# Modulation sums moved beside the merge, the attention's slots filled in another order, and three hand-overs and the first loads reordered

## The chip, the cores and the metric

The kernel runs on one core of a Trainium2 chip. The metric is device time in microseconds (us) of one launch; before the change it is 2489.1 us, the median of 3 runs (2488.27 to 2489.74). The core's engines run in parallel, each through its own list of instructions in order: PE (TensorE: matmuls), DVE (VectorE), ACT (ScalarE), POOL (GpSimd), and SP, which here only issues DMA transfers. An instruction that waits for another engine holds everything behind it on its own engine.

## The reference, cut to what matters

One layer over 512 latent tokens of width 1024, with 256 context tokens that share all weights:

```
mx = (silu(c) @ w_ada + b_ada)                     # six modulation vectors: sh1, sc1, g1, sh2, sc2, g2
px = split((x * (1 + sc1) + sh1) @ w_in)           # all input projections; pc the same for the context
ox_hg  = HGRN2 recurrence over 8 heads             # branch A
ox_cv  = Conformer convolution, 31 taps            # branch B
qx, kx = rope(rms_norm(q)), rope(rms_norm(k))      # branch C: 8 query heads, 4 key/value heads
ox_att = softmax(q k^T / sqrt(128)) v              # over 512 + 256 keys
mix = (sig(z0) * hg_out(ox_hg) + sig(z1) * conv_out(ox_cv) + sig(z2) * (ox_att @ w_att_o)) @ w_out
x = LN(alpha * x + g1 * mix)
q = (x * (1 + sc2) + sh2) @ wq                     # PEER: top 16 of 128 + 128 keys, 8 heads
act = gelu(u_tab[expert] . x);  y = sum(gate * act * v_tab[expert])
x = LN(alpha * x + g2 * y)
```

Of the modulation vectors, sh1 and sc1 are needed at the start; g1, sh2, sc2 and g2 only after the attention.

## The kernel before, in words

Every product is done in float32 as three passes over a weight split in two parts: `wload` starts a 512 KB transfer into `wraw` (three buffers in rotation), ACT writes the upper part `whi` in two halves, and DVE or POOL subtracts it to give the lower part `wlo`. `mm3` then issues three matmuls per 128 rows (lines L142 to L144), so a product of 512 columns has 24 matmuls.

The order of weights is one list, `todo`, filled by `want(...)`. `fetch_next()` takes the next entry, if fewer than three stand ready, and issues its load and its conversion at that place of the program; `feed(...)` hands over the first that is ready, and if there is none it issues the load and the conversion on the spot. An entry `('ada', a)` is a load alone, of 512 KB of the transposed `w_ada`: it takes a `wraw` buffer until it is used.

The stages, in order of time:

- Start (0 to 39 us): sh1 and sc1 from `w_ada`, by matmuls; loads on SP's queue, small constants on ACT's.
- HGRN2 heads and convolution (to about 600 us), then norm and the first output product with its gate.
- The merge loop (656 to 744 us), 8 steps `j`: a gate product `('in', Z_MG + KT + j)`, a sigmoid on ACT, a product `('conv', j)`, a multiplication on DVE (`ms`), an addition on POOL (`mix`).
- Attention (745 to about 1062 us): 32 slots, one for each of 8 heads and 4 blocks of queries. `slot(n, early, late, mid)` does in this order: softmax scaling of slot n (`P`), the softmax of n+1, the scores of n+2 (`S`), the steps in `early`, the transposes of `P` (`pt`), the steps in `late`. The steps fill PE's time with the projections of the next group's heads: `key`, `value` and `query` are generators whose `yield` marks where a step ends. A group is 8 slots (two query heads over one key head): g = 0, 1, 2 prepare the next, g = 3 computes the third branch's merge gates instead (`mgate`).
- Into the same slots the modulation sums are dealt: `adas()` multiplies a 128x1024 piece of `w_ada` with silu(c) and adds it up on DVE, one instruction for each of 32 pieces, plus an addition of the bias after every four.
- Output projection, PEER queries and top-k (`decodes` and `best` on DVE), with dense products of the expert table as filler (`next_item`). `SUBS` says which engine makes `wlo` for which table.
- Gate loop (1445 to 1640 us): one-hot matrices on DVE, matmuls `pg`, dense products as filler from a generator `run`. Then the dense stage (1656 to 2430 us): `weigh(n)` multiplies activations and gates, split in `ph` and `pl`, and products add up into `acc`.

PSUM tiles named `mm` come from a pool of two in the attention: a third one waits until the first has been read.

Of the kernel before, what the change touches and what calls it, by code (L numbers as in the profile page):

```python
# [94 lines left out]
def body(tc, I, O):  # L95
# [65 lines left out]
    nc.scalar.dma_start(cc, I['cc'])  # L161
    nc.scalar.dma_start(bada, I['b_ada'])
    A.activation(silc, cc, AF.Sigmoid)
# [44 lines left out]
    hgn = cst.tile([128, 1], F32, name="hgn")  # L208
    nc.scalar.dma_start(hgn, I['hg_g'])
    dw = cst.tile([128, KT, 31], F32, name="dw")  # L210
    nc.scalar.dma_start(dw, I['dw'])
    chan = {}
    for n in ('cb', 'clg', 'clb'):
        chan[n] = cst.tile([128, KT], F32, name=n)
        nc.scalar.dma_start(chan[n], I[n])
    hcs = ExitStack()
# [32 lines left out]
    def want(*ws):  # L249
        for w in ws:  # L250
            todo.append(w)

    def run(*gens):
        for g in gens:
            for _ in g:
                pass
# [36 lines left out]
    want(('in', Z_G + H - 1), ('in', Z_MG + 6), ('in', Z_MG + 7))  # L293
    want(*[('hg', j) for j in range(KT)])
    for j in range(KT):
        want(('in', Z_MG + KT + j), ('conv', j))
    want(*[('in', z) for z in (Z_AK, Z_AQ, Z_AV, Z_AQ + 1)])
# [344 lines left out]

    for t in (0, 0, 0, 0, 1, 0, 1, 0, 1, 0):
        next(first[t])
    lbl = cst.tile([128, 2, H], F32, name="lbl")
    nc.scalar.dma_start(lbl, I['lbl'])
# [91 lines left out]
    for j in range(KT):  # L738
# [8 lines left out]
        go(ln)  # L747
    run(ln)
    for j in range(KT):
        ps = pmm.tile([128, T], F32, name="mm")  # L750
        p_ = product(ps, feed('in', Z_MG + KT + j), xhl, 4)
        go(p_)
        fetch_next()
        go(p_)
        s = mp.tile([128, T], F32, name="ms", bufs=2)
        A.activation(s, ps, AF.Sigmoid)
        ps = pmm.tile([128, T], F32, name="mm")
        p_ = product(ps, feed('conv', j), uhl, 4)
        go(p_)
        fetch_next()  # L760
        go(p_)
        fetch_next()
        V.tensor_mul(s, ps, s)
        G.tensor_add(mix[j], mix[j], s)
# [57 lines left out]
    NS = NB + NBC  # L822
    steps = [a for j in range(32) for a in ((j,) if j % 4 < 3 else (j, None))]
    for g in range(3):
        for n, z in ((0, Z_AK + g + 1), (2, Z_AQ + 2 * g + 2), (3, Z_AV + g + 1), (2, Z_AQ + 2 * g + 3), (3, None)):
            want(*[('ada', a) for a in steps[:n] if a is not None])
            del steps[:n]
            if z is not None:
                want(('in', z))
    mg = [('in', Z_MG + 16 + j) for j in range(KT)]  # L830
    for n, m in ((2, 0), (3, 1), (3, 2), (2, 3)):
        want(*[('ada', a) for a in steps[:n] if a is not None])
        del steps[:n]
        want(*(mg[m:m + 1] if m < 3 else mg[3:]))
    want(*[('att', j) for j in range(KT)], ('u', 0))
# [6 lines left out]
    def key(g):  # L842
# [15 lines left out]
        for (x, n, o_), (zg, sq) in zip(SEG, zs):  # L858
            k_ = ap_.tile([128, T], F32, name="qT", bufs=2)[:, :n * 128]
            if n == NB:  # L860
                rope(k_, zg)
                V.tensor_mul(k_, k_, bcast1(rs[:, :NB], n))
            else:
                V.tensor_mul(k_, zg[:, :n * 128], bcast1(rs[:, NB:], n)[:, :n * 128])
            sl = slice(o_ * 128, (o_ + n) * 128)
            split(kT[0][:, sl], kT[1][:, sl], k_)
            yield
# [109 lines left out]

    silb = oat[:, 6:8, :].rearrange("p a t -> p (a t)")
    nc.scalar.dma_start(silb, rowbc(I['c_row'], D))
    for i in range(2):  # L980
        sgb = ap_.tile([128, T + TC], F32, name="P")[:, :T]
        A.activation(sgb, silb[:, i * T:i * T + T], AF.Sigmoid)
        V.tensor_mul(silb[:, i * T:i * T + T], silb[:, i * T:i * T + T], sgb)

    def adas():

        for j in range(32):
            raw = feed('ada', j)[:].rearrange("p k e -> p (k e)")
            V.tensor_tensor_reduce(out=raw, in0=raw, in1=silb, scale=1.0, scalar=0.0, op0=ALU.mult, op1=ALU.add,
                                   accum_out=mod[:, 16 + j, 0:1])  # L990
            yield
            if j % 4 == 3:
                m = mod[:, 13 + j:17 + j, 0]
                V.tensor_add(m, m, bada[:, 13 + j:17 + j])
                yield

    a_ = adas()

# [4 lines left out]
    fetch_next()  # L1003
    go(qa, k_, qa, k_, qa, k_, qa)
    fetch_next()
# [25 lines left out]
    for g in range(4):  # L1031
        n = 8 * g
        if g == 3:
            slot(n, (qb,), (qb, a_, a_))
            m_ = chain([mgate(j) for j in range(KT)])
            for h in range(2):
                for i, nm in ((0, "kh"), (1, "kl")) if h == 0 else ((0, "vh"), (1, "vl")):
                    t_ = ap_.tile([128, T + TC] if h == 0 else [128, NS, 128], F32R, name=nm)
                    ohl[i][h] = t_[:, :T] if h == 0 else t_[:, :NB, :].rearrange("p n e -> p (n e)")
            slot(n + 1, (m_, m_), (m_, m_, a_, a_, a_), (do(begin, 2 * g + 1),))  # L1040
            slot(n + 2, (m_, m_), (m_, m_, a_, a_, a_))
            slot(n + 3, (m_, m_), (m_, m_, a_, a_))
            slot(n + 4, (), (m_, m_))
            for l in range(5, 8):
                slot(n + l, (m_, m_, m_), (m_, m_))
            for h in range(2):
                split(ohl[0][h], ohl[1][h], oat[:, h, :])
            run(m_)
            break
        k_, qa, v_ = key(g + 1), query(2 * g + 2), value(g + 1)  # L1050
        slot(n, (qb,), (qb, k_, a_))
        slot(n + 1, (k_,), (k_, a_), (do(begin, 2 * g + 1),))
        slot(n + 2, (k_, qa), (qa, qa, a_, a_))
        slot(n + 3, (qa,), (k_, k_, qa, a_))
        slot(n + 4, (qa,), (v_, a_))
        slot(n + 5, (v_,), (v_, a_), (do(begin, 2 * g + 2),))
        qb = query(2 * g + 3)
        slot(n + 6, (v_, v_, qb), (qb, a_))
        slot(n + 7, (qb,), (qb, a_, a_))
    wo = [[xp.tile([128, KT, T], F32R, name=n) for n in ("xh", "xl")]]  # L1060
# [358 lines left out]
    TR = [3, 3, 3, 3, 3]  # L1419
    SUBS.update(u=(V, V))  # L1420
    for n in TR[:2]:
        for _ in range(n):
            next_item(pmm, "mm")
        decodes()
    sm = tk.tile([128, NB, H], F32, name="gsum", bufs=1)
# [138 lines left out]
    RUN = 4 * (len(items) - pos[1] - 3)  # L1564
    order_rows()
    for j in range(steps):
        new = onehots(j + 1) if j + 1 < steps else None
# [37 lines left out]

    fetch(('v', 0))
    for _ in run:
        pass
    fetch(('v', 1))
    weigh(0, arun[:, 0, :])  # L1610
    homes.append(pp)
# [180 lines left out]
```

## Time and profile before

| what | value |
| --- | --- |
| median of 3 runs | 2489.1 us |
| the profiled execution | 2489.15 us |
| its span in the trace | 2487.1 us |
| PE busy | 2357.9 us, 95% of the span |
| DVE, ACT, POOL busy | 78%, 42%, 26% |
| mean granted clock of PE | 0.982 |

The span is the time from the first to the last recorded instruction; 2.05 us lie around it. "Busy" counts the time in which an engine has an instruction under way. The granted clock is a share of full speed (2.4 GHz; the lower level is 1.2 GHz). What ends an engine's idle time is the instruction named behind "<-".

### The profile page before, as it was taken

Reading aid. Unit: us, or ns where it says so; the run is one execution under the profiler, and the core shown is the slowest. Engines: PE = TensorE matmul, PEld = TensorE weight load, DVE = VectorE, ACT = ScalarE, POOL = GpSimd, SP = SyncE. Lnnn points to the kernel's source line nnn. Section 1 sums busy time; section 2 is a strip of 40 time slices with the busy share of each in tenths; the row PEclk is TensorE's granted clock in tenths of the full one; section 3 lists DMA queues with packets and bytes.
Section 4 is the critical chain, followed back from the end, with each engine's and each line's share of the span. In section 5 each row is a group of like instructions: output and inputs, shape, how many; then the busy total and the mean of one; then the engine's idle time right before and its main releaser. Section 6 shows DMA issues by size and latency. Waiting matters only on the chain.

```text
span 2487.1 us, 34757 instructions
## 1 busy us (share of the span) xinstructions
PE 2357.9 (95%) x12547; PEld 2033.9 (82%) x12547; DVE 1928.1 (78%) x3728; ACT 1045.3 (42%) x2298; POOL 651.5 (26%) x558
## 2 busy tenths in 40 slices
PE   7999999999999888899999999999989999999997
PEld 3888888887877777687899889987767889898886
DVE  7788888887524666665799779968878878889886
ACT  5544444434323343543466645543333333333333
POOL 6000000003220000031588300113222344444432
PEclk9999999999999999999999999999999999999999
DMA  6211111112322222432332368999999989998962
GB/s 240 70 60 60 60 60 60 60 60 68 101 95 62 92 86 85 136 110 102 112 111 96 110 221 312 315 318 318 309 376 362 333 324 358 327 342 318 335 221 100
DMA packets 156973, 452.66 MB, mean 182 GB/s; under 512 B 16256, under 2 KB 60672, under 8 KB 154624
## 3 DMA queue, kind: packets, MB, share of 16 engines
q1 hardware_dynamic: 106976, 278.33, 32.4%
q0 software_dynamic: 36864, 134.23, 15.4%
q10 hardware_dynamic: 12960, 37.87, 4.0%
q8 instruction: 99, 1.62, 0.3%
q14 instruction: 74, 0.61, 0.1%
HBM read 411.77 MB, written 37.03 MB: 180 GB/s over the span
## 4 chain that ended last, share of the span: by engine, by line
PE 60%; DVE 23%; DMA 6%; ACT 6%; issue 4%; POOL 1%; ACTq 0%; DVEq 0%; POOLq 0%; SPq 0%
PE mm L142 12%; PE mm L144 12%; PE mm L143 12%; DVE wlo L131 5%; DVE raw L1491 3%; PE acc L142 2%; PE acc L143 2%; PE acc L144 2%; PE pa L142 2%; PE pa L144 2%; PE pa L143 2%; DMA wraw<-in_v_dram 2%; PE pg L1541 2%; ACT whi L129 2%; PE sc L466 2%
## 5 line engine op out<-in xcount | busy, mean ns | idle before, releaser
L131 DVE TENSOR_TENSOR wlo<-wraw,whi 128x512 fp32r<-128x512 f32 x686 | 458.4, 710 | 191.1 <-ACT whi L129 181.3
L142 PE MATMUL mm<-xh,wlo 128*128 128x512 f32 (+1 forms) x1456 | 561.9, 386 | 26.9 <-DVE wlo L131 11.5
L143 PE MATMUL mm<-xl,whi 128*128 128x512 f32 (+1 forms) x1456 | 542.8, 373 | 1.2 <-POOL xl L327 0.8
L144 PE MATMUL mm<-xh,whi 128*128 128x512 f32 (+1 forms) x1456 | 542.8, 373 | 0.0
L129 ACT ACTIVATE whi<-wraw 128x512 fp32r<-128x512 f32 x784 | 448.8, 621 | 108.9 <-PE mm L144 28.4
L142 PEld LDWEIGHTS mm<-xh,wlo 128*128 128x128 f32 x1456 | 277.4, 191 | 61.2 <-DVE vl L138 12.0
L142 PE MATMUL acc<-whi,pl 128*128 128x512 f32 x756 | 300.1, 397 | 28.8 <-DVE pl L138 24.7
L144 PEld LDWEIGHTS mm<-xh,whi 128*128 128x128 f32 x1456 | 276.6, 190 | 37.6
L143 PEld LDWEIGHTS mm<-xl,whi 128*128 128x128 f32 x1456 | 277.5, 191 | 34.3 <-DVE xl L327 1.8
L143 PE MATMUL acc<-wlo,ph 128*128 128x512 f32 x756 | 301.1, 398 | 2.0 <-DVE wlo L131 0.9
L144 PE MATMUL acc<-whi,ph 128*128 128x512 f32 x756 | 297.9, 394 | 0.0
L1480 POOL DMA_INDIRECT raw<-in_u_dram,idx x128 | 148.2, 1158 | 478.9 <-DVE act L1491 421.0
L1480 POOL DMA_INDIRECT raw<-in_v_dram,idx x128 | 160.7, 1256 | 189.3 <-DVE ttok L1499 152.4
L142 PEld LDWEIGHTS acc<-whi,pl 128*128 128x128 f32 x756 | 143.5, 190 | 67.3 <-DVE pl L138 22.7
L561 DVE SCALAR_TENSOR_TENSOR u<-up,dw,u 128x512 f32<-128x512 f32 x240 | 179.6, 748 | 4.9
L137 ACT ACTIVATE ph<-a 128x384 fp32r<-128x384 f32 x94 | 49.4, 525 | 310.3 <-DVE a L1600 256.2
L143 PEld LDWEIGHTS acc<-wlo,ph 128*128 128x128 f32 x756 | 143.4, 190 | 41.2 <-DVE wlo L131 12.5
L144 PEld LDWEIGHTS acc<-whi,ph 128*128 128x128 f32 x756 | 143.7, 190 | 28.7
L1499 DVE SCALAR_TENSOR_TENSOR ttok<-raw,act,ttok 128x1024 f32<-128x1024 f32 x127 | 162.9, 1283 | 3.1
L131 POOL TENSOR_TENSOR wlo<-wraw,whi 128x512 fp32r<-128x512 f32 x98 | 136.2, 1411 | 97.7 <-ACT whi L129 95.8
L142 PE MATMUL pa<-xh,wlo 128*128 128x384 f32 x456 | 154.0, 338 | 3.3 <-DVE wlo L131 3.2
L144 PE MATMUL pa<-xh,whi 128*128 128x384 f32 x456 | 153.6, 337 | 0.0
(422 smaller groups left out, 4237.1 us busy)
## 6 DMA issues: line engine op xcount, KB each, us to landing
wraw<-in_uT_dram SPq DMA_DIRECT2D x128, 512.0 KB
wraw<-in_v_dram SPq DMA_DIRECT2D x128, 512.0 KB
wraw<-in_w_in_dram SPq DMA_DIRECT2D x96, 512.0 KB
gd<-gs ACTq DMA_DIRECT2D x16, 1536.0 KB
gr<-gd SPq DMA_DIRECT2D x60, 288.0 KB
wraw<-in_w_adaT_dram SPq DMA_DIRECT2D x32, 512.0 KB
wraw<-in_wq_dram SPq DMA_DIRECT2D x16, 512.0 KB
ad<-a ACTq DMA_DIRECT2D x39, 192.0 KB
```

What stands on the lines that cost most here:

```text
L129: A.activation(hi, r, AF.Copy)
L131: subs[i].tensor_sub(lo, r, hi.bitcast(F32))
L137: A.activation(hi, src, AF.Copy)
L142: P.matmul(out, ll, rh, start=first, stop=False)
L143: P.matmul(out, lh, rl, start=False, stop=False)
L144: P.matmul(out, lh, rh, start=False, stop=last)
L466: P.matmul(x_.ps[:, b, :], x_.KM[:, b * 128:(b + 1) * 128], ap3(x_.QP, T + b * 128, [2 * w_, 64 // w_], [w_ - T, 2], [1, w_]), start=True, ...
L561: V.scalar_tensor_tensor(acc, up[:, i:i + T], dw[:, j, i:i + 1], acc, op0=ALU.mult, op1=ALU.add)
L1480: G.indirect_dma_start(out=r, out_offset=None, in_=I['u'] if n < NS_ else I['v'], in_offset=bass.IndirectOffsetOnAxis(ap=idx0[:, n % NS_:n ...
L1491: V.tensor_tensor_reduce(out=r, in0=r, in1=ttok, scale=1.0, scalar=0.0, op0=ALU.mult, op1=ALU.add, accum_out=act[:, s_:s_ + 1])
L1499: V.scalar_tensor_tensor(ysb, r, act[:, s_:s_ + 1], ysb, op0=ALU.mult, op1=ALU.add)
L1541: P.matmul(ps[:, i, :], o3[:, q_, :, i], o1[:, i, :], start=q_ == 0, stop=q_ == 1)
```

## The change

- First loads: the loads of `bada`, `hgn`, `dw` and three small vectors, issued on ACT's queue at once, are issued after the first step of the first modulation product.
- Modulation sums: `adas()`, the load of `c` as a row and its silu stand ahead of the merge loop, and each of its 8 steps takes four sums and one bias addition. `silb` has a tile of its own. The weights' list has the pieces between the merge's weights.
- Attention: `key` gets one more `yield` (behind the rotation, ahead of its broadcast), the steps are dealt in another order, and no sums are among them.
- Hand-overs: the switch `SUBS.update(u=(V, V))` comes after three more items; five pieces of `run` are done ahead of the gate loop; `weigh(0, ...)` is issued after six of the remaining pieces of `run` and not after all.

```diff
-    nc.scalar.dma_start(bada, I['b_ada'])
-    nc.scalar.dma_start(hgn, I['hg_g'])
-    nc.scalar.dma_start(dw, I['dw'])
-        nc.scalar.dma_start(chan[n], I[n])
...
+    steps = [a for j in range(32) for a in ((j,) if j % 4 < 3 else (j, None))]
     for j in range(KT):
-        want(('in', Z_MG + KT + j), ('conv', j))
+        for n, w in ((0, ('in', Z_MG + KT + j)), (2, ('conv', j)), (3, None)):
+            want(*[('ada', a) for a in steps[:n] if a is not None])
+            del steps[:n]
+            want(*([w] if w else []))
...
-    for t in (0, 0, 0, 0, 1, 0, 1, 0, 1, 0):
+    for i, t in enumerate((0, 0, 0, 0, 1, 0, 1, 0, 1, 0)):
         next(first[t])
+        if i == 0:
+            for t_, n in ((bada, 'b_ada'), (hgn, 'hg_g'), (dw, 'dw'), *((chan[n], n) for n in ('cb', 'clg', 'clb'))):
+                nc.scalar.dma_start(t_, I[n])
...
+    a_ = adas()
     for j in range(KT):
         ps = pmm.tile([128, T], F32, name="mm")
         p_ = product(ps, feed('in', Z_MG + KT + j), xhl, 4)
         go(p_)
         fetch_next()
-        go(p_)
+        go(p_, a_)
+        fetch_next()
+        go(a_)
         s = mp.tile([128, T], F32, name="ms", bufs=2)
         A.activation(s, ps, AF.Sigmoid)
         ps = pmm.tile([128, T], F32, name="mm")
         p_ = product(ps, feed('conv', j), uhl, 4)
-        go(p_)
+        go(p_, a_)
         fetch_next()
-        go(p_)
+        go(p_, a_, a_)
         fetch_next()
         V.tensor_mul(s, ps, s)
         G.tensor_add(mix[j], mix[j], s)
...
                 rope(k_, zg)
+                yield
                 V.tensor_mul(k_, k_, bcast1(rs[:, :NB], n))
...
-            slot(n + 1, (m_, m_), (m_, m_, a_, a_, a_), (do(begin, 2 * g + 1),))
+            slot(n + 1, (m_, m_), (m_, m_), (do(begin, 2 * g + 1),))
...
-        slot(n, (qb,), (qb, k_, a_))
-        slot(n + 1, (k_,), (k_, a_), (do(begin, 2 * g + 1),))
-        slot(n + 2, (k_, qa), (qa, qa, a_, a_))
-        slot(n + 3, (qa,), (k_, k_, qa, a_))
-        slot(n + 4, (qa,), (v_, a_))
-        slot(n + 5, (v_,), (v_, a_), (do(begin, 2 * g + 2),))
+        slot(n, (qb,), (qb, k_))
+        slot(n + 1, (k_,), (k_,), (do(begin, 2 * g + 1),))
+        slot(n + 2, (k_, qa, qa), (qa, qa, k_))
+        slot(n + 3, (k_, k_), (v_,))
+        slot(n + 4, (), (v_,))
+        slot(n + 5, (qa, v_), (v_, qa), (do(begin, 2 * g + 2),))
         qb = query(2 * g + 3)
-        slot(n + 6, (v_, v_, qb), (qb, a_))
-        slot(n + 7, (qb,), (qb, a_, a_))
+        slot(n + 6, (v_, qb), (qb,))
+        slot(n + 7, (qb,), (qb,))
...
     TR = [3, 3, 3, 3, 3]
-    SUBS.update(u=(V, V))
     for n in TR[:2]:
         for _ in range(n):
             next_item(pmm, "mm")
+        SUBS.update(u=(V, V))
         decodes()
...
     order_rows()
+    LEAD = 5
+    for _ in range(LEAD):
+        next(run)
+    RUN -= LEAD
...
     fetch(('v', 0))
+    for _ in range(6):
+        next(run, None)
+    weigh(0, arun[:, 0, :])
     for _ in run:
         pass
     fetch(('v', 1))
-    weigh(0, arun[:, 0, :])
```

ACT in the merge loop, before: `L756 ms<-mm` is the sigmoid of a gate product, `whi<-wraw` the conversion of a weight's two halves.

```order
L129 ACTIVATE whi<-wraw 128x512 x10
L756 ACTIVATE ms<-mm 128x512
L129 ACTIVATE whi<-wraw 128x512 x4
L756 ACTIVATE ms<-mm 128x512
L129 ACTIVATE whi<-wraw 128x512 x4
```

The same place of the changed kernel, where the sigmoid of a gate product is L781 and the two L756 are those of `silb`:

```order
L129 ACTIVATE whi<-wraw 128x512 x4
L753 DMA silb<-in_c_row_dram 128x1024
L756 ACTIVATE ms<-silb 128x512 x2
L129 ACTIVATE whi<-wraw 128x512 x2
L781 ACTIVATE ms<-mm 128x512
L129 ACTIVATE whi<-wraw 128x512 x2
L781 ACTIVATE ms<-mm 128x512
L129 ACTIVATE whi<-wraw 128x512 x4
```

Before, ten halves (five weights) are converted ahead of the first sigmoid, so the four behind a sigmoid belong to weights of the next step or later. In the changed kernel six halves (three weights) stand ahead of it, two behind the first sigmoid and four behind the second and each later one: from the second step on these four are the weight `conv` of this step and the gate weight of the next, since each step uses six entries of the list and has four `fetch_next()`.

PE in a group's slots, before, from the transposes of slot n+3 to the first score matmul in slot n+4: `zg,swap` is a rotation, `ident,ars` the broadcast of the key's norm (four for the tokens, two for the context), `S` scores.

```order
L945 MATMUL pt<-ident,P 128x128 x6
L810 MATMUL mm<-zg,swap 128x512
L819 MATMUL mm<-ident,ars 128x128 x6
L810 MATMUL mm<-zg,swap 128x512
L142 MATMUL S<-kh,ql 128x512
```

The answering place of the changed kernel, from the end of slot n+2 to the first matmul behind the transposes of slot n+3:

```order
L144 MATMUL mm<-xh,whi 128x512
L835 MATMUL mm<-zg,swap 128x512
L142 MATMUL S<-kh,ql 128x512
L143 MATMUL S<-kl,qh 128x512
L144 MATMUL S<-kh,qh 128x512
L142 MATMUL S<-kh,ql 128x256
L143 MATMUL S<-kl,qh 128x256
L144 MATMUL S<-kh,qh 128x256
L844 MATMUL mm<-ident,ars 128x128 x6
L962 MATMUL pt<-ident,P 128x128 x6
L142 MATMUL mm<-xh,wlo 128x512
```

Before, two rotations (key, query) and the broadcast between them follow each other with nothing else; after, the key's rotation comes behind a projection, six score matmuls stand between it and the broadcast, and the query's rotation has moved on to slot n+5.

POOL at the last heads of the top-k, before: `pay` are the candidates' indices, `eq` comparisons for the decoding.

```order
L1409 TENSOR_TENSOR pay<-ii 128x4x3
L1409 TENSOR_TENSOR pay<-ii 128x4x6
L1409 TENSOR_TENSOR pay<-ii 128x4x8
L1350 TENSOR_TENSOR eq<-eb,pay 128x800 x6
L1480 DMA raw<-in_u_dram,idx_13377 128x1024 x128
```

And in the changed kernel:

```order
L1406 TENSOR_TENSOR pay<-ii 128x4x3
L1406 TENSOR_TENSOR pay<-ii 128x4x6
L1406 TENSOR_TENSOR pay<-ii 128x4x8
L131 TENSOR_TENSOR wlo<-wraw,whi 128x512 x6
L1347 TENSOR_TENSOR eq<-eb,pay 128x800 x6
```

Six subtractions (three weights) have come to POOL between the last `pay` and the comparisons; they stood on DVE before.

## Rows read from the trace of the kernel before

**Rows 1.** The page: the span, and PE's busy time (share, instructions).

```profile
span 2487.1 us, 34757 instructions
...
PE 2357.9 (95%) x12547; PEld 2033.9 (82%) x12547; DVE 1928.1 (78%) x3728; ACT 1045.3 (42%) x2298; POOL 651.5 (26%) x558
```

**Rows 2.** Busy time by stretches: merge, one group's attention, gate loop.

```profile
core 0: us, PE busy (x) PEld busy (x) DVE busy (x) ACT busy (x) POOL busy (x), PEclk, DMA share, GB/s
678.00:700.00 22.00, 22.00 (x97) 17.86 (x96) 4.96 (x8) 5.67 (x10) 5.84 (x4) 1.00 0.27 96
...
800.00:872.00 72.00, 63.20 (x328) 51.98 (x328) 46.98 (x97) 28.12 (x59) 3.34 (x3) 0.93 0.26 88
...
1550.00:1600.00 50.00, 50.00 (x415) 47.96 (x413) 47.16 (x66) 26.80 (x40) 5.74 (x5) 1.00 0.92 315
```

**Rows 3.** Timeline of one merge step: start, duration, engine, line, operation.

```profile
669.11 1.30 POOL L131 TENSOR_TENSOR wlo<-wraw,whi 128x512 fp32r<-128x512 f32 x1
...
671.77 0.39 PE L144 MATMUL mm<-xh,whi 128*128 128x512 f32 x1
...
672.20 0.60 ACT L756 ACTIVATE ms<-mm 128x512 f32<-128x512 f32 x1 [4.78 <-PE mm L144]
672.69 1.14 ACT L129 ACTIVATE whi<-wraw 128x512 fp32r<-128x512 f32 x2
673.35 1.30 DVE L131 TENSOR_TENSOR wlo<-wraw,whi 128x512 fp32r<-128x512 f32 x2 [5.34 <-ACT whi L129]
```

**Rows 4.** A weight's load in the merge: SP's issue; GB/s in 1.1 us slices from 656.

```profile
658.12 0.33 SPq L124 DMA_DIRECT2D wraw<-in_w_in_dram  x1
...
GB/s 0 0 30 331 115 0 0 63 309 104 0 0 0 11 249 216 0 60 309 123 0 0 0 0 249 227 0 19 320 138 0 0 0 0 138 339 0 0 238 246
```

**Rows 5.** Timeline of POOL in the start, with DVE busy beside it.

```profile
20.86 1.74 POOL L131 TENSOR_TENSOR wlo<-QP,whi 128x512 fp32r<-128x512 f32 x1
```

**Rows 6.** Groups of DVE in 745 to 1062: the modulation sums.

```profile
L989 DVE CUSTOM_DVE_ANT_0 wraw<-wraw,oat 128x1024 f32<-128x1024 f32 x32 | 38.4, 1216 | 0.0
```

**Rows 7.** PE's waits in 745 to 800: releaser, total us, times, longest.

```profile
PE mm L142 <- ACT asq L792: 1.4, 1, 1.4
```

**Rows 8.** PE's waits in 800 to 872, one group of slots.

```profile
PE mm L142 <- DVE vl L138: 3.2, 1, 3.2
PE mm L819 <- ACT asq L792: 1.6, 1, 1.6
PE mm L810 <- DVE qT L862: 1.4, 1, 1.4
PE pt L945 <- DVE P L937: 1.4, 1, 1.4
PE mm L819 <- DVE asq L812: 0.8, 1, 0.8
```

**Rows 9.** Timeline of PE behind the longest of these waits.

```profile
843.95 0.63 PE L144 MATMUL mm<-xh,whi 128*128 128x512 f32 x1
```

**Rows 10.** PE's waits in 1002 to 1062, the last group.

```profile
PE mm L142 <- DVE wlo L131: 3.6, 1, 3.6
PE S L142 <- DVE ql L138: 2.7, 1, 2.7
PE pt L945 <- DVE P L937: 2.6, 2, 2.2
PE mm L801 <- DVE asq L812: 0.8, 1, 0.8
```

**Rows 11.** PE's waits in 1378:1390, 1440:1462 and 1640:1665.

```profile
PE mm L142 <- DVE wlo L131: 5.1, 1, 5.1
...
PE pg L1541 <- issue: 4.4, 1, 4.4
...
PE acc L142 <- DVE pl L138: 4.6, 1, 4.6
```

**Rows 12.** Timeline of POOL at the first of these waits.

```profile
1382.16 1.53 POOL L1409 TENSOR_TENSOR pay<-ii 128x64 f32<-128x64 f32 x7 [3.53 <-DVE ii L1402]
```

**Rows 13.** SP's waits in the first 12 us.

```profile
SPq L307 <- DMA bada<-in_b_ada_dram: 4.4, 1, 4.4
```

More of the change, by code (lines that the diff above doesn't have):

```diff
@@ L748, in body, with adas @@
     run(ln)
+    silb = mp.tile([128, D], F32, name="silb")
+    nc.scalar.dma_start(silb, rowbc(I['c_row'], D))
+    for i in range(2):
+        sgb = mp.tile([128, T], F32, name="ms", bufs=2)
+        A.activation(sgb, silb[:, i * T:i * T + T], AF.Sigmoid)
+        V.tensor_mul(silb[:, i * T:i * T + T], silb[:, i * T:i * T + T], sgb)
+    def adas():
+        for j in range(32):
+            raw = feed('ada', j)[:].rearrange("p k e -> p (k e)")
+            V.tensor_tensor_reduce(out=raw, in0=raw, in1=silb, scale=1.0, scalar=0.0, op0=ALU.mult, op1=ALU.add,
+                                   accum_out=mod[:, 16 + j, 0:1])
+            yield
+            if j % 4 == 3:
+                m = mod[:, 13 + j:17 + j, 0]
+                V.tensor_add(m, m, bada[:, 13 + j:17 + j])
+                yield
+    a_ = adas()
     for j in range(KT):
@@ L822, in body @@
     NS = NB + NBC
-    steps = [a for j in range(32) for a in ((j,) if j % 4 < 3 else (j, None))]
     for g in range(3):
[L825 to L834, printed above, removed]
+        want(*[('in', z) for z in (Z_AK + g + 1, Z_AQ + 2 * g + 2, Z_AV + g + 1, Z_AQ + 2 * g + 3)])
+    want(*[('in', Z_MG + 16 + j) for j in range(KT)])
     want(*[('att', j) for j in range(KT)], ('u', 0))
@@ L861, in key @@
                 rope(k_, zg)
+                yield
                 V.tensor_mul(k_, k_, bcast1(rs[:, :NB], n))
@@ L976, in do @@
         yield
[L978 to L997, printed above, removed]
     for _ in range(3):
@@ L1003, in body @@
     fetch_next()
-    go(qa, k_, qa, k_, qa, k_, qa)
+    go(qa, k_, qa, k_, k_, qa, k_, qa)
     fetch_next()
@@ L1033, in body @@
         if g == 3:
-            slot(n, (qb,), (qb, a_, a_))
+            slot(n, (qb,), (qb,))
             m_ = chain([mgate(j) for j in range(KT)])
@@ L1039, in body @@
                     ohl[i][h] = t_[:, :T] if h == 0 else t_[:, :NB, :].rearrange("p n e -> p (n e)")
-            slot(n + 1, (m_, m_), (m_, m_, a_, a_, a_), (do(begin, 2 * g + 1),))
-            slot(n + 2, (m_, m_), (m_, m_, a_, a_, a_))
-            slot(n + 3, (m_, m_), (m_, m_, a_, a_))
+            slot(n + 1, (m_, m_), (m_, m_), (do(begin, 2 * g + 1),))
+            slot(n + 2, (m_, m_), (m_, m_))
+            slot(n + 3, (m_, m_), (m_, m_))
             slot(n + 4, (), (m_, m_))
```

## The prediction

> **What bounds the kernel now.** I read the page first: PE is busy for 2357.9 of 2487.1 us [rows 1], so 129.2 us are left in which it idles, and nothing is won anywhere but in those or in stretches at the lower clock. Busy time by stretches then tells where each edit lands [rows 2]. In the merge PE works for all 22.00 of 22.00 us at full clock, so there is nothing to win there and every wait is new; DVE is busy for 4.96 of 22.00. In a group of attention slots (72 us) PE is busy for 63.20, so 8.8 us are idle, and the granted clock is 0.93. In the gate loop PE is busy for 50.00 of 50.00, DVE for 47.16, with a DMA share of 0.92. PE's waits name who is late [rows 7, 8, 10, 11], and the timeline of a merge step gives the durations of a weight's conversion [rows 3].
>
> The sum is made against the profiled execution (2489.15 us; span 2487.1 and 2.05 around it). It stands 0.05 us above the median, so a difference carries over to the median as it is.
>
> **The change part by part.**
>
> *First loads.* SP's fourth load waits 4.4 us for the transfer of `bada`, which shares its lane [rows 13]. That wait goes, but the six moved transfers now stand on ACT ahead of its second conversion, and POOL's subtractions (1.74 us each while DVE works [rows 5]) go on behind one another. I take 0, with 1.5 us of loss and 1.5 of gain as bounds.
>
> *Sums beside the merge.* 32 sums of 1.216 us [rows 6] come to DVE, four a step: 4.9 us in a step of 11, where DVE is now busy for a quarter. Their own time is therefore hidden. What isn't hidden is the order of weights. Six entries a step and four `fetch_next()` empty the store of ready weights in the second step; from then on the weight `conv` of a step is converted behind that step's sigmoid, as ACT's order in the section on the change shows. Before, it had been converted long before, and PE went from the gate product into the conv product without a break. Now PE waits for this chain, counted from the start of the last gate matmul at 671.77 [rows 3]: the sigmoid starts 0.43 later (672.20), the conversion 0.49 after that (672.69), the first half of `wlo` 0.66 after that (673.35) and takes 0.65 (half of 1.30). PE can go on at 674.0, 2.28 us behind the last start instead of one matmul's spacing of 0.23 (22.00 us for 97 of them [rows 2]): 2.05 us lost a step, 7 steps, 14.4 us.
>
> The gate weight of the next step is converted in the same place. Its buffer comes free when POOL has subtracted the second half of `conv` (1.30 us [rows 3], from 2.1 to 3.4 us behind the mark). A load takes about 3.0 us: issued at 658.12, its bytes flow in the slices up to about 661.5 [rows 4]. Conversion and first subtraction take 0.6 and 0.65. That gives 3.5 + 3.0 + 1.25 = 7.75 us behind the mark, and the conv product ends at 2.28 + 24 x 0.23 = 7.8: just in time. Two loads of pieces follow it on the queue and can share its bandwidth, so I add 0.4 us a step, 2.6 in all: **+17 us**. The lower bound is 14 without this. The upper takes POOL's 1.74 us for 1.30 and half as long again for the load, 1.9 us a step, 13 more, so 28.
>
> The Trainium skill ("SBUF — State Buffer", section "SBUF: two separate sides") states that a DVE operation with two inputs in SBUF and a GpSimd operation that reads SBUF exclude one another for the whole instruction. The sums are such operations, and POOL's subtraction of `conv` would start up to 1.216 us later behind one of them. The trace agrees in kind: 1.30 us alone and 1.74 beside a busy DVE. By that rule the next gate weight would be late by 1.2 us more in each of 7 steps, and the merge would cost 25 us, inside the bounds.
>
> *Attention, before the slots.* ACT no longer waits there for the row of `c`, and PE's 1.4 us behind `asq` [rows 7] go: **-1.4** (0 to -3).
>
> *Attention, three groups.* In one group PE waits 3.2 us for `vl`, 1.6 and 0.8 for `asq`, 1.4 for `qT` and 1.4 for `P`, 8.4 together [rows 8]; the other two groups repeat this within 0.6 us. The chain of `qT`, `asq` arises because two rotations and a broadcast stand back to back and the pool of two PSUM tiles makes each wait for the reader of the last. In the new order the six score matmuls and a projection lie between the parts (about 1.0 us of score matmuls, three of 512 columns and three of 256; 24 of 0.23 for a product). What I still find late when I follow the new order by hand: 0.4 us for `P`, 1.2 for the PSUM tile of the value's product, 0.3 more behind it. The wait for `vl` arises because its copy on ACT stands behind the exponential of the next slot, and a projection behind the copy; now the transposes of `P`, the query's statistics and six score matmuls stand between, and I find 0.45 left. So 2.35 of 8.4 stay: -6.0 a group, -18 in three. The clock falls behind such waits: a matmul that takes 0.39 us [rows 3] takes 0.63 there [rows 9]. A clock of 0.93 over 72 us [rows 2] is 10 us at the lower level, and some 5 us of work lost per group at most. That it returns with the waits is likely, how much is not known: nothing and 12 us in three groups are the bounds, and I take 4, near the lower end, since some waits stay. **-22**; bounds -8 (half of the waits only move) and -30.
>
> *Attention, last group.* 3.6 + 2.7 + 2.6 + 0.8 = 9.7 us [rows 10], most of it behind subtractions on DVE that wait for a late weight. The pieces of `w_ada` that share the three buffers are gone, so loads start earlier. I leave 1.2 us and add 2 of clock: **-10.5** (-4 to -14).
>
> *Three weights' subtractions to POOL.* PE waits 5.1 us for `wlo` on DVE [rows 11], behind the top-k. On POOL the first can start when `pay` ends, 1382.16 + 1.53 = 1383.69 [rows 12], and takes 1.30 to 1.74. PE starts at 1385.0 to 1385.4 instead of 1387.4: **-2.2** (-1 to -4). The comparisons behind them on POOL come up to six subtractions later; DVE reads their results only after the next three products, over 10 us on, which hides it. Without that cover it would cost the same 8 us back.
>
> *Five pieces ahead of the gate loop.* PE waits 4.4 us for the first one-hot matrices [rows 11]; 30 more matmuls fill it. The pieces are taken from the loop, where PE is the longer one by 50.00 to 47.16, so the loop shortens: **-4.4** (-1 to -5.5).
>
> *`weigh(0)` earlier.* PE waits 4.6 us for `pl` [rows 11], the end of a chain of weight, gates and split. With the remaining pieces of `run` behind it on PE this chain runs beside them; a PSUM tile may still be late by 0.6: **-4** (-1 to -6.5).
>
> Sum: 0 + 17 - 1.4 - 22 - 10.5 - 2.2 - 4.4 - 4 = -27.5, so 2489.15 - 27.5 = 2461.6 us, and 2461.6 for the median. Call it 2461.5.
>
> **Rivals.**
>
> *The merge costs 28 us and more*: the load of the next gate weight is late in each step, and PE's clock falls with the waits. For it: two loads behind it on the queue and POOL's slower subtraction; against it: the calculation gives just in time, and waits of 2 us in 13 are shorter than those behind which the clock fell. Time: 2489.1 - 44.5 + 30 = about 2475.
>
> *The attention's waits only move*: other steps wait for the same two PSUM tiles and for ACT's exponential. For it: DVE's scaling, maximum and ACT's exponential stay in each slot; against it: 38.4 us of DVE's work [rows 6] leave this stage. Half of the attention's 34 us is gone: about 2478.5.
>
> *The gate loop and the dense stage give back what the last two hand-overs win*: DMA share 0.92 there [rows 2]. Then the 8.4 us stay away: about 2470.
>
> *Slower than before*: in the merge each weight is loaded only when its buffer comes free, and both products of a step wait for the whole of it, 3.0 of load, 1.3 of conversion and 1.3 of subtraction. This would be 5.6 us twice in 7 steps, 78 us, and 2489.1 - 44.5 + 78 = 2522.6. It decides from 44.5 / 7 = 6.4 us a step. Against it: SP issues the load of `conv` a whole gate product (5.5 us) ahead of its use.
>
> **How the numbers follow.** My forecast has 0.5, the dearer merge 0.13, the moved waits 0.15, the hand-overs given back 0.14, the slower case 0.08. A measurement of this kernel can tell about 0.2%, 5 us, from no change. The first four cases lie below 2484; the moved waits together with a dear merge would come to within 5 us, for which I set 0.04, taken from those two. So faster 0.88, same 0.04, slower 0.08. The range runs from 2446, where most of the gains reach their bounds, to 2479, which takes in the three middle rivals.
>
> **What would show it.** In the trace after: in each merge step from the second a wait of PE of about 2 us ahead of the conv product, released by `wlo` on DVE; no `vl` wait of 3 us and no chain of `asq` and `qT` in 800 to 1010; a last group with waits under 2 us; the three waits of the tail [rows 11] at 3, 0 and 0.6 us. I am wrong if the conv product follows the gate product without a break, if its wait is over 3 us, or if the waits between 750 and 1060 still come to over 25 us.

## The result, and the profile after

The changed kernel takes 2463.1 us (median of 4 runs, 2457.3 to 2469.7), the kernel before 2489.4 beside it: ratio 0.9897, 95% interval 0.9875 to 0.9919. It is faster by about 1%, 1.6 us from the forecast of 2461.5. Its profiled execution is one of the longer ones, 2469.7 us. From its page, the span and PE's busy time, to be read beside [rows 1]:

```profile
span 2467.8 us, 34756 instructions
...
PE 2356.6 (95%) x12547; PEld 2028.7 (82%) x12547; DVE 1937.8 (79%) x3722; ACT 1044.3 (42%) x2298; POOL 667.5 (27%) x564
```

PE's work has stayed the same; 111 us are left idle where 129 were. Where they went is best seen in the lengths of stages, each counted from the start of one matmul in the trace to the start of another, in us (profiled executions):

| stage | before | changed | difference |
| --- | --- | --- | --- |
| to the first product on the tokens | 39.6 | 38.6 | -1.0 |
| merge, first to last conv matmul | 82.9 | 108.3 | +25.3 |
| from there to the first score matmul | 32.2 | 34.0 | +1.8 |
| first to last matmul `S<-kh` | 344.7 | 306.1 | -38.5 |
| PEER queries to the first one-hot matmul | 273.7 | 271.6 | -2.1 |
| from there to the first dense accumulation (`acc`) | 203.5 | 192.8 | -10.7 |
| first to last accumulation | 816.3 | 822.1 | +5.8 |

The stages not listed differ by 0.1 us or less, and these sum to -19.4, the difference of the two spans within 0.1. (The keys' buffers serve in a later product too, so the stretch of `S<-kh` reaches 71 us beyond the last score matmul, alike in all kernels.)

PE's waits in the changed merge loop and just behind it, 656 to 773 us. Before, the loop had no wait at all, and the one for `ms` behind it was 0.9 us:

```profile
PE mm L142 <- DVE wlo L131: 16.5, 9, 2.0
PE mm L142 <- DVE ms L788: 2.8, 1, 2.8
```

Nine waits for `wlo`: seven of 2.0 us, ahead of the conv products, and two of 1.3 and 1.4 us ahead of gate products. One of them in the timeline (start, duration, engine, line, operation), to be read beside [rows 3]:

```profile
715.64 0.39 PE L144 MATMUL mm<-xh,whi 128*128 128x512 f32 x1
718.02 0.75 PE L142 MATMUL mm<-uhi,wlo 128*128 128x512 f32 x1 [1.99 <-DVE wlo L131]
718.56 0.63 PE L143 MATMUL mm<-og,whi 128*128 128x512 f32 x1
...
716.13 0.60 ACT L781 ACTIVATE ms<-mm 128x512 f32<-128x512 f32 x1 [6.09 <-PE mm L144]
716.62 1.14 ACT L129 ACTIVATE whi<-wraw 128x512 fp32r<-128x512 f32 x2
717.27 0.69 DVE L131 TENSOR_TENSOR wlo<-wraw,whi 128x512 fp32r<-128x512 f32 x1 [2.45 <-ACT whi L129]
717.88 1.22 DVE L763 CUSTOM_DVE_ANT_0 wraw<-wraw,silb 128x1024 f32<-128x1024 f32 x1
717.89 2.35 POOL L131 TENSOR_TENSOR wlo<-wraw,whi 128x512 fp32r<-128x512 f32 x1 [4.16 <-ACT whi L129]
```

ACT idles for 6.09 us, converts nothing, then does the sigmoid, and only then the weight that PE needs next: the conv product starts 2.38 us behind the last gate matmul (the forecast said 2.28). Behind the wait a matmul takes 0.63 us. Busy time by stretches, to be read beside [rows 2]; the columns are those given there:

```profile
678.00:700.00 22.00, 18.76 (x80) 14.68 (x80) 14.61 (x20) 3.76 (x7) 6.78 (x3) 1.00 0.67 222
700.00:722.00 22.00, 18.02 (x63) 13.72 (x62) 13.37 (x19) 4.42 (x8) 6.91 (x3) 0.84 0.54 186
```

22.00 of 22.00 has become 18 to 19, and in one of the two stretches the granted clock is 0.84.

PE's waits in one group of slots (870 to 932 us) and in the last group (994 to 1054), which answer to [rows 8] and [rows 10]:

```profile
PE pt L962 <- DVE P L954: 2.0, 3, 1.2
PE mm L142 <- DVE qT L879: 0.8, 1, 0.8
PE mm L903 <- DVE vl L138: 0.2, 1, 0.2
...
PE pt L962 <- DVE P L954: 1.2, 1, 1.2
PE S L142 <- DVE ql L138: 1.0, 1, 1.0
```

3.0 us in the group where 8.4 and more were, 2.2 in the last where 9.7 were. The places of [rows 11], in 1360:1380, 1420:1460 and 1620:1650:

```profile
PE mm L142 <- POOL wlo L131: 2.7, 1, 2.7
...
PE sk L1451 <- DVE ef L1447: 0.4, 1, 0.4
...
PE acc L142 <- ACT whi L129: 1.0, 1, 1.0
PE acc L142 <- ACT a L1287: 0.6, 1, 0.6
PE acc L143 <- DVE wlo L131: 0.2, 1, 0.2
```

The first wait is 2.7 where 5.1 were, the second is gone, the third has fallen from 4.6 to 0.6, and 1.2 more come a little later.

### The profile page after: what moved, and what is told of

Same layout as the page of the kernel before. It is cut to its first block, busy times and chain, and to the rows that moved or that the text cites. A ratio compares the mean times of both kernels' runs of the same rounds, so it can differ in the third digit from the quotient of the medians.

```text
span 2467.8 us, 34756 instructions
## 1 busy us (share of the span) xinstructions
PE 2356.6 (95%) x12547; PEld 2028.7 (82%) x12547; DVE 1937.8 (79%) x3722; ACT 1044.3 (42%) x2298; POOL 667.5 (27%) x564
## 4 chain that ended last, share of the span: by engine, by line
PE 57%; DVE 25%; DMA 6%; ACT 5%; issue 4%; POOL 2%; ACTq 0%; DVEq 0%; SPq 0%; POOLq 0%
PE mm L142 13%; PE mm L144 12%; PE mm L143 12%; DVE wlo L131 6%; DVE raw L1488 3%; DVE ttok L1496 3%; DMA wraw<-in_v_dram 3%; ACT whi L129 2%; PE sc L466 2%; PE pg L1538 2%; ACT ph L137 2%; DMA wraw<-in_uT_dram 2%; PE acc L142 1%; PE acc L143 1%; PE acc L144 1%
## 5 line engine op out<-in xcount | busy, mean ns | idle before, releaser
L131 DVE TENSOR_TENSOR wlo<-wraw,whi 128x512 fp32r<-128x512 f32 x680 | 453.1, 708 | 186.1 <-ACT whi L129 184.2
L144 PEld LDWEIGHTS mm<-xh,whi 128*128 128x128 f32 x1456 | 275.0, 189 | 37.2
L131 POOL TENSOR_TENSOR wlo<-wraw,whi 128x512 fp32r<-128x512 f32 x104 | 149.2, 1457 | 123.0 <-ACT whi L129 116.6
```

What stands on the lines that cost most here:

```text
L131: subs[i].tensor_sub(lo, r, hi.bitcast(F32))
L144: P.matmul(out, lh, rh, start=False, stop=last)
```

## The experiments

All are edits of the changed kernel unless said otherwise. Stages are counted as in the table above; "slots" is the stretch of `S<-kh`, and the times are medians.

**The changed kernel again.**

> The changed kernel unaltered, run again beside the experiments, since its four times lie in two groups (2457 and 2469 us). Both theories: times in the same two groups, 2456 to 2470. If the two groups come from where the lower clock falls, the stretches at the lower clock in a profile near 2457 are some 10 us shorter in sum than in the one near 2469; if they come from the loads of the dense stage, the difference of about 10 us lies behind 1650 us, and the merge and attention take the same time in both.

2464.8 us (6 runs, 2460.6 to 2470.6), merge 108.9, slots 306.2, accumulation 818.6. With the four runs above, ten times lie between 2457 and 2471. No profile caught an execution near 2457, so where the scatter comes from isn't told. The mean granted clock alone is not it: of the first four executions, 2457.9 and 2468.3 us both had 0.990. Differences under 5 us below are therefore read from stages and waits, not from the time.

**The conv weight taken ahead of the sigmoid.**

> Only the order on ACT is changed: in a merge step the weight of the conv product is taken (and converted) ahead of the sigmoid of the gate product. Theory (the conversion stands behind the sigmoid): the wait ahead of the conv product falls from 2.3 to under 0.5 us in 7 steps, the merge from 108 to 90 us or less, the whole by 14 to 20 us. Rival (the weight's load is late, or the sums on DVE hold up its subtraction): the wait stays near 2 us, the whole within 4 us of the changed kernel.

```diff
+        cv = feed('conv', j)
         s = mp.tile([128, T], F32, name="ms", bufs=2)
         A.activation(s, ps, AF.Sigmoid)
         ps = pmm.tile([128, T], F32, name="mm")
-        p_ = product(ps, feed('conv', j), uhl, 4)
+        p_ = product(ps, cv, uhl, 4)
```

2454.2 us (ratio to before 0.9844, 0.9823 to 0.9866), merge 93.8 instead of 108.9. PE's waits in its merge and just behind it:

```profile
PE mm L142 <- DVE wlo L131: 7.9, 8, 1.6
PE mm L142 <- DVE ms L789: 1.2, 1, 1.2
```

One line moved, and 15 us of the merge are back, a little more than half of the loss: the conversion behind the sigmoid did cost PE its time. PE's waits fall from 16.5 us to 7.9, and from 678 to 744 us the granted clock is 1.00. The expected size wasn't reached, though. The whole gains 10.6 us, not 14 to 20, the merge stays over 90, and waits of 0.6 to 1.6 us stay ahead of conv and gate products. What ACT now waits for is the load itself, issued 4.5 us earlier (SP's issue, ACT's conversion):

```profile
704.38 0.33 SPq L124 DMA_DIRECT2D wraw<-in_w_conv_o_dram  x1
...
708.88 1.15 ACT L129 ACTIVATE whi<-wraw 128x512 fp32r<-128x512 f32 x2 [5.34 <-DMA wraw<-in_w_conv_o_dram]
```

**Two more places to fetch.**

> Two more places per merge step at which the next entry of the weights' list is loaded and converted, one ahead of the sigmoid and one behind the start of the conv product, so that weights are converted a product ahead. Theory: both the wait ahead of the conv product (2.3 us in 7 steps) and the smaller one ahead of some gate products (1.6 us in 2) go, the merge takes 83 to 86 us instead of 108, the whole 20 to 25 us less. Rival (loads at 0.65 of the DMA engines, or sums and subtractions on DVE and POOL hold each other up): waits of 1 us and more stay in most steps and the merge stays over 95 us.

```diff
         go(a_)
+        fetch_next()
         s = mp.tile([128, T], F32, name="ms", bufs=2)
...
         p_ = product(ps, feed('conv', j), uhl, 4)
+        fetch_next()
         go(p_, a_)
```

2503.7 us (1.0048, 1.003 to 1.0065), slower than before the change. The theory (a merge of 83 to 86) failed. Merge 135.7: 13 waits of up to 3.8 us. DVE and SP in one step of it:

```profile
702.82 1.29 DVE L131 TENSOR_TENSOR wlo<-wraw,whi 128x512 fp32r<-128x512 f32 x2 [5.59 <-ACT whi L129]
704.03 1.22 DVE L763 CUSTOM_DVE_ANT_0 wraw<-wraw,silb 128x1024 f32<-128x1024 f32 x1
...
712.32 0.69 DVE L131 TENSOR_TENSOR wlo<-wraw,whi 128x512 fp32r<-128x512 f32 x1 [5.12 <-ACT whi L129]
...
704.14 1.47 SPq L269 DMA_DIRECT2D wraw<-in_w_adaT_dram  x2
706.43 0.33 SPq L124 DMA_DIRECT2D wraw<-in_w_conv_o_dram  x1
```

The subtraction of a weight now stands on DVE ahead of the sums of pieces that were loaded before it. DVE idles for 5 us until the weight is there, the sums behind it can't free their buffers, and so the next three loads start only after it, one behind the other (704.14 to 706.43), the last of them for the product that PE is ready for at 710.8. A place to fetch earlier in the program made the loads later. The same happens once more behind the loop, where the last `ms` stands on DVE behind the subtractions of three weights of the attention:

```profile
809.81 0.77 PE L142 MATMUL mm<-xh,wlo 128*128 128x512 f32 x1 [14.06 <-DVE ms L790]
```

The stage from the merge to the first score matmul takes 46.5 us, where the changed kernel run again took 33.9. Merge and this stage together make the whole loss of 39 us.

**Another order in the list.**

> The changed kernel with another order in the merge's list (gate weight, one piece, conv weight, three pieces) and two more places to load and convert, so that a weight's buffer comes free behind a sum, not behind the weight ahead of it, and each weight is converted a product ahead. Theory (with three buffers for six loads a step, what counts is which load waits for which release): the waits fall under 0.5 us each and the merge takes 83 to 88 us, the whole 2440 to 2450. Rival (six loads of 512 KB in 11 us are too many for three buffers in any order, since two rounds of load and use don't fit into one step): waits of 1 us and more stay in most steps and the merge takes 92 us or more.

```diff
-        for n, w in ((0, ('in', Z_MG + KT + j)), (2, ('conv', j)), (3, None)):
+        for n, w in ((0, ('in', Z_MG + KT + j)), (1, ('conv', j)), (4, None)):
...
```

The steps of the loop are dealt to match, with six fetches, and the conv weight is taken ahead of the sigmoid here too. 2494.6 us (1.0012, 0.9998 to 1.0026), merge 127.8, with waits of 3.6 to 4.8 us ahead of six gate products, and 45.6 us from there to the first score matmul. In the trace the issue of three pieces takes SP 7.18 us from 705.66, since each waits for a buffer, and the next gate weight's load stands behind them (714.76). The rival's number; but the next run shows that six loads a step aren't too many in themselves.

**Buffers of their own for the pieces.**

> The changed kernel with four buffers of their own for the pieces of the modulation weights, in the memory that the first output product leaves free ahead of the merge loop; the merge's weights have the three buffers and the look-ahead of the kernel before for themselves. Theory (the merge loses by the shared list and buffers, not by the sums on DVE or the bytes): merge 83 to 85 us as before the change, the whole 2438 to 2446. Rival (1.2 us sums and POOL's subtractions exclude one another, or six loads a step are too much for the DMA engines): waits of 1 us and more ahead of products, merge over 90 us.

```diff
+            raw = ar.tile([128, KT, 128], F32, name="araw", bufs=4)
+            nc.sync.dma_start(raw, source('ada', asrc.pop(0))[0])
+            araws.append(raw)
...
-            raw = feed('ada', j)[:].rearrange("p k e -> p (k e)")
+            raw = araws.pop(0)[:].rearrange("p k e -> p (k e)")
...
+            aload()
```

The memory of `ohi` and `olo` goes to a pool that closes ahead of the merge loop, and the merge's list and its three fetches a step are those of before. 2439.1 us (ratio 0.979, 0.9771 to 0.9808): 26 us better than the changed kernel's 2464.8, 54 better than the kernel before, which took 2493.4 beside it. The merge takes 82.9, as before the change:

```profile
683.00:705.00 22.00, 22.00 (x97) 17.89 (x96) 20.12 (x29) 5.65 (x11) 7.80 (x4) 1.00 0.78 287
```

The same 32 sums, the same bytes (287 GB/s, a DMA share of 0.78), DVE busy for 20 of 22 us, and PE waits for nothing. Neither the bytes nor the sums' time on DVE made the merge's loss; the shared three buffers and the shared order did. Which of these two counts for more isn't told, since this edit undoes both at once.

**No sums.**

> The 32 modulation sums and their 16 MB of loads are left out (the modulation vectors behind the attention are then wrong); the list holds only the merge's weights. It prices the sums in their new place. Theory: the merge takes 83 us as before the change, and the rest is as in the changed kernel, so 25 us less, about 2440. Rival (the sums cost only the conversions' order, and the same loss would stay with any list that short): the merge stays over 95 us.

2439.5 us (0.9789), merge 82.9, slots 306.2. What the sums cost in their new place is thus the 25 us of the merge, and the kernel with its own buffers does them at no cost that can be told (2439.1).

**Sums in the slots, new order.**

> The changed kernel with the modulation sums dealt into the attention's slots again, as before the change, but with the new order of projections and the extra hand-over in the key. Theory (order of projections ends most waits in three groups; the sums' loads make those of the last group): merge 83 us; the 32 slots 306 us in the changed kernel and 345 before, here 318 to 326; the whole about 2452. Rival (the slots gain because the sums leave DVE and the three buffers): slots over 332 us, the whole over 2462.

2473.9 us (0.9914), merge 82.9, slots 341.1: the rival. PE's waits in one group (880 to 952), and what DVE does ahead of the longest:

```profile
PE pt L945 <- DVE P L937: 6.8, 3, 2.8
PE S L142 <- DVE ql L138: 0.5, 1, 0.5
PE mm L886 <- DVE vl L138: 0.2, 1, 0.2
...
883.11 1.22 DVE L990 CUSTOM_DVE_ANT_0 wraw<-wraw,oat 128x1024 f32<-128x1024 f32 x1
...
884.25 1.22 DVE L990 CUSTOM_DVE_ANT_0 wraw<-wraw,oat 128x1024 f32<-128x1024 f32 x1
...
885.59 0.62 DVE L937 TENSOR_SCALAR P<-P,ssum 128x768 f32<-128x768 f32 x1
```

The waits for `asq` and `qT` are gone with the new order, and `vl` is down to 0.2, but `P` waits in their place behind two sums. Another dealing of the sums might do better; this one keeps 3.6 of 38.5 us.

**Old order, sums in the merge.**

> The changed kernel with the old order of projections in the slots and no extra hand-over in the key; the sums stay in the merge. Theory: the waits for asq, qT and vl come back in three groups, 5 to 6.5 us each, and the last group stays as in the changed kernel: slots 322 to 328 us, the whole 16 to 22 us above the changed kernel, 2478 to 2485. Rival (the sums on DVE made these waits): slots under 314 us, the whole within 8 us of the changed kernel.

2473.1 us (0.9907), slots 315.2, between theory and rival. PE's waits in one group (880 to 945), to be read beside [rows 8]:

```profile
PE mm L142 <- DVE vl L138: 1.9, 1, 1.9
PE mm L835 <- DVE qT L878: 1.4, 1, 1.4
PE mm L844 <- DVE asq L837: 0.8, 1, 0.8
```

Of 8.4 us, 4.1 come back: `qT`, the `asq` of DVE and a part of `vl` belong to the order. The wait for `P`, that for ACT's `asq` and the rest of `vl` had been the sums'.

**Loads without the sums' time** (edit of the kernel before).

> The kernel before the change with each of the 32 sums replaced by a copy of one column of the loaded piece (the modulation vectors behind the attention are then wrong); the loads, the buffers and the order of projections stay. It tells what of the attention's gain is DVE's time and what is the buffers'. Theory (DVE's time makes the waits for P, for asq on ACT and a part of that for vl in three groups, the buffers those of the last group): slots 326 to 334 us, where they are 345 before and 315 with the old order and no sums. Rival (the loads in the three buffers make all of it): slots over 340 us.

```diff
-            V.tensor_tensor_reduce(out=raw, in0=raw, in1=silb, scale=1.0, scalar=0.0, op0=ALU.mult, op1=ALU.add,
-                                   accum_out=mod[:, 16 + j, 0:1])
+            V.tensor_copy(mod[:, 16 + j, 0:1], raw[:, :1])
```

2464.4 us (0.9891), slots 319.8, better than expected. The waits in a group are those of the last run to 0.1 us; in the last group (975 to 1035) they stay:

```profile
PE S L142 <- DVE ql L138: 3.6, 1, 3.6
PE mm L142 <- DVE wlo L131: 2.4, 1, 2.4
PE mm L801 <- DVE asq L812: 0.8, 1, 0.8
...
```

So of the 29.5 us that the slots gain when the sums leave (344.7 to 315.2), 24.9 are DVE's time, and 4.6 more come when the loads leave too. These 4.6 are a balance. Counted from the first score matmul of a group, the last group (up to its last slot's scores) takes 68.4 us before, 61.9 here and 52.7 with the old order and no sums: 6.5 us are DVE's time there and 9.2 the loads'. Against this the first group takes 56.3 here and 61.1 in that kernel; why isn't told.

**Without the five pieces; `weigh(0)` late; first loads and POOL's subtractions undone.**

> The changed kernel without the five pieces of dense products ahead of the gate loop. Theory: the wait of 4.4 us ahead of the first one-hot product comes back and the stage from there to the first dense accumulation is unchanged otherwise: 3 to 5 us more in all. Rival (the loop or the dense stage behind it sets the time): within 2 us.

> The changed kernel with the first weighting of the activations issued again after all dense products of the gate stage. Theory: PE waits 4 to 5 us for the split activations again and works some 2 us at the lower clock behind it: 4 to 7 us more up to the first accumulation, and as much at the end. Rival (the dense stage, near its loads' limit, gives it back): the first accumulation 4 to 7 us later, but the end within 2 us.

> The changed kernel with two parts undone that lie far apart in time: the first loads issued in the old order, and the switch that gives the subtractions of the expert table back to DVE in its old place, so that six of them stand on DVE behind the top-k. Theory: the first matmul on the tokens starts 39.6 us behind the start, not 38.6 to 39.3 (the first loads gain 0 to 1 us); the wait behind the top-k is 5.1 us and not 2.7, and the stage from the PEER queries to the gate loop takes 273.7 us and not 271.6; the whole 2 to 3 us more, which the scatter of the times hides. Rival (the wait is shared out over later products anyway): the stage takes 271.6 us still.

PE's waits at the three places, in the three kernels in this order:

```profile
PE pg L1538 <- issue: 4.4, 1, 4.4
```

```profile
PE acc L142 <- DVE pl L138: 4.6, 1, 4.6
```

```profile
PE mm L142 <- DVE wlo L131: 5.1, 1, 5.1
```

Each wait comes back as it was. Without the pieces the stage up to the first accumulation takes 199.5 instead of 192.8, and the whole 2469.9; with the late weighting 196.9, and 2468.1; with POOL's subtractions undone the PEER stage takes 274.9 instead of 271.6, and the whole 2465.7. In that last kernel the first product on the tokens starts at 39.2 us, within the 38.6 to 40.0 of all kernels: the first loads change nothing that can be told. The three times lie 5.1, 3.3 and 0.9 us above the changed kernel's 2464.8, in the right direction but within its scatter; the waits and stages are what shows the steps.

## Why the prediction was right

The time, 2463.1, came out by a sum whose terms were partly off in opposite directions; that it lies within 1.6 us of the forecast is in part luck. The two profiled executions differ by 19.4 us, 8 less than the forecast's 27.5; beside the experiments the medians differ by 28 (2493.0 and 2464.8).

- **The merge, +17, measured +25.3.** The mechanism is as forecast: the conversion behind the sigmoid (undone in part by one moved call, 15 us), the gate weight late in some of the steps (two here, two to four in the other profiles of the same loop). The waits for `wlo` come to 16.5 us, 13.9 ahead of conv products and 2.7 ahead of gate products; the sum had 14.4 and 2.6. (Its 2.28 us is 2.23 by its own terms, 0.43 + 0.49 + 0.66 + 0.65, which makes 14.0.) What the term lacks is the clock: some 30 matmuls of 0.63 us instead of 0.39 behind these waits (6 to 7 us), and 0.84 granted in the stretch of 700 to 722 us. The forecast had this in the rival "the merge costs 28 us and more" at 0.13 and argued that waits of 2 us are too short for it. They are not: behind four of the seven the granted clock fell, behind three it did not. The trace of before had a case too, waits of 1.6, 0.8 and 1.4 us close together [rows 8] and then 0.50 granted from 818.3 to 821.7 us.
- **Ahead of the slots, -1.4, measured +1.8.** The wait for ACT's `asq` went, but the first key product now waits 2.8 us for DVE's multiplication `ms` of the last merge step, where 0.9 us were; with buffers of their own it is 0.9 again. This isn't fixed by the order: in the three last kernels above, which have the same merge, that wait is 1.0 to 1.2 us and the stage takes 30.6 to 30.8, as forecast. What decides it isn't told.
- **Attention, -22 and -10.5, measured -38.5.** By groups, the three give -21.3 and the last -17.1. The step that failed is the cause. The forecast put the waits of the three groups down to the order of rotations, the pool of two PSUM tiles and ACT's exponential, and gave DVE's 38.4 us of sums no share. The four combinations tell: order alone gives 3.6 (sums in the slots; 2.1 of it in the three groups), moving the sums alone 29.5, both 38.5. So the -22 is right in size by luck. The sums stood ahead of the scaling of `P` and of the maximum `smax` on DVE, and what waits for these came late. DVE and PE in the kernel before:

```profile
809.04 1.22 DVE L989 CUSTOM_DVE_ANT_0 wraw<-wraw,oat 128x1024 f32<-128x1024 f32 x1
...
810.38 0.62 DVE L937 TENSOR_SCALAR P<-P,ssum 128x768 f32<-128x768 f32 x1
...
811.14 0.85 PE L945 MATMUL pt<-ident,P 128*128 128x128 f32 x6 [1.38 <-DVE P L937]
```

The term that was sized too small is the clock, for which the forecast took 4 + 2 us. Busy time from the first slot's scores to the last slot's, before, with the old order and no sums, and changed (columns as in [rows 2]):

```profile
776.00:1048.70 272.70, 235.49 (x1201) 193.07 (x1199) 176.46 (x357) 115.09 (x225) 11.03 (x10) 0.94 0.28 93
...
803.10:1046.30 243.20, 227.33 (x1200) 189.26 (x1199) 139.93 (x287) 116.85 (x225) 11.01 (x10) 0.96 0.11 37
...
802.20:1036.30 234.10, 221.50 (x1200) 182.96 (x1199) 139.98 (x287) 115.12 (x225) 11.03 (x10) 0.99 0.12 39
```

PE's idle time falls from 37.2 to 12.6 us, by 24.6, where the forecast's waits were 26.5. The other 14 us are busy time, for the same matmuls: the granted clock rises from 0.94 to 0.99. The order is worth 9.0 once the sums are gone; 3.3 of it are idle time and the rest the clock (0.96 to 0.99). In the last group the loads' 9.2 us are near the forecast's 10.5; what it left out there is DVE's time, 6.5.

- **The three hand-overs, -2.2, -4.4 and -4, measured -2.1 and -10.7** for the second and third together (6.7 and 4.1 in the runs without one of them): right, the second somewhat larger, since the lower clock behind its wait went too (0.76 granted in 1453 to 1460 us before, 1.00 in 1430 to 1445 after).
- **First loads, 0**: nothing that can be told.
- **The dense stage.** Its rival (8.4 us given back) is not borne out as a whole: accumulation takes 818.6 to 822.1 in the two profiles and 816.3 before. 2 to 6 us may have been given back; over all the runs here the stage scatters from 816.4 to 825.0, so this stays open.
- **The slower rival** named a merge in which weights are loaded only when a buffer comes free and PE waits for the whole of it. The change doesn't do that, but the kernel with two more fetches comes near it: merge 135.7 and a whole of 2503.7. The condition that the forecast set against it, the conv load a product ahead, is what that kernel breaks.

## What to carry to other kernels

When work goes into an order that other work shares, look at what it displaces there, not at its own time: 38 us of sums cost 25 us in the merge through three shared buffers and a list that ran dry, and nothing with four buffers of their own. An engine that is busy for two thirds of a stage can still set its time: what counts is what stands behind each added instruction in that engine's queue, and who waits for that. And waits cost more than their own length where the granted clock falls behind them: 14 of the 38.5 us that the attention gained are the clock. Fetching earlier helps only as long as the fetched thing doesn't stand ahead, on an engine in order, of what would free the next buffer.

## What was not expected of the hardware

Beside the sums, POOL's operations in the merge take much longer, and the sums too. Groups of DVE and POOL in 661 to 766 us of the changed kernel:

```profile
L763 DVE CUSTOM_DVE_ANT_0 wraw<-wraw,silb 128x1024 f32<-128x1024 f32 x30 | 48.7, 1641 | 4.4 <-DMA wraw<-in_w_adaT_dram 4.2
...
L789 POOL TENSOR_TENSOR mix<-mix,ms 128x512 f32<-128x512 f32 x7 | 15.4, 2205 | 53.6 <-DVE ms L788 53.6
L131 POOL TENSOR_TENSOR wlo<-wraw,whi 128x512 fp32r<-128x512 f32 x7 | 15.4, 2204 | 29.4 <-ACT whi L129 29.4
```

A sum takes 1.64 us in the mean where it took 1.216 in the slots [rows 6], and POOL's subtraction 2.20 instead of 1.30 [rows 3], 0.9 us more. The Trainium skill ("SBUF — State Buffer", section "SBUF: two separate sides") says of two such operations that they exclude one another for the whole instruction; the longer times agree with it, and the forecast's estimate by it was up to 1.2 us. In time it cost little: the kernel with buffers of its own has nearly as long operations (1.60 and 2.10 us in the mean) and a merge of 82.9 us. The forecast's +25 "by that rule" met the merge's +25.3 by chance: gate products waited in two of seven steps, for 2.7 us in all, and what the sum lacked was the clock.
